# Mean over 8192 rows on one core: four small unused loads behind the first six groups, and a different last wait of SyncE

## The chip, the core and the metric

The kernel runs on one core of a Trainium2 chip. The metric is the device time of one execution in microseconds (us), so lower is better. The profile of one execution gives a slightly shorter figure, the span from the first to the last instruction of the program: 626.3 us, where that execution took 628.09 us.

## The reference

```python
def setup_inputs():
    return {"x": np.random.randn(8192, 8192).astype(np.float32)}

def reference(x):
    return np.mean(x, axis=0)
```

All 8192 rows of an 8192-column matrix of float32 are averaged: 268.44 MB are read from memory and 32 KB are written. Each number that is read enters one addition.

## The kernel before

The rows are read in 64 groups of 128 (G = 64, P = 128); a group is one row per partition, 4 MB. `bufs` holds six groups: slots 0 to 3 take the loads, slot 4 (`both`) and slot 5 (`acc`) the sums. VectorE adds groups until a few are left, TensorE adds the last ones over the partitions with a matrix of 1/8192, ScalarE and VectorE copy the results out of PSUM, and five small stores write them.

All loads are issued by SyncE, through one helper. A load is a DMA; it tells of its end through one of eight semaphores, taken in turn. The helper takes away the dependencies that the new load has on earlier loads (`declare_no_dep`), apart from two that it names in every second load, `over`.

```python
    def landed(*inss):
        nop = tc.keep_in_program_order(nc.sync.nop()).ins
        for o in inss:
            tc.add_manual_dep(nop, o.name, sync, reason="SyncE waits")

    def load(dst, src):
        ins = tc.keep_in_program_order(nc.sync.dma_start(out=dst, in_=src)).ins
        k = len(loads)
        over = loads[k - 8:k - 6] if k >= 8 and k % 2 == 0 else []
        tc.declare_no_dep(ins, group="loads", keep=over, reason="the reader of the buffer waited")
        for o in over:
            tc.add_manual_dep(ins, o.name, sync, reason="covers the next load too")
        tc.add_to_no_dep_group("loads", ins)
        loads.append(ins)
        return ins
```

The start: a part of a late group that is kept in `early`, four groups in one load, two groups in a second, and another part of a late group in `early`. Two large additions on VectorE bring the six groups down to one. The loop then loads two groups at a time into two free slots and adds them.

```python
    load(early[:, 5 * F:], rows(G - 4)[:, 14 * F:])
    first, second = load_rows(0, 0, 4), load_rows(4, 4, 2)
    load(early[:, :5 * F], rows(G - 1)[:, 9 * F:14 * F])
    add(bufs[:, 2:4, :], bufs[:, 2:4, :], bufs[:, 0:2, :], [first])
    add(bufs[:, 4:6, :], bufs[:, 4:6, :], bufs[:, 2:4, :], [second])
    add(acc, acc, both, [])
    # ... (warm-up of ScalarE)
    g = 6
    while g < G - 8:
        u = (g + 2) % 4
        dma = load_rows(g, u, 2)
        add(both, bufs[:, u, :], bufs[:, u + 1, :], [dma])
        add(acc, acc, both, ahead)
        # ... (GpSimd adds what lies in early at g = 24 and 32)
        g += 2
```

The end, cut: the last groups are loaded in pieces, summed by TensorE, copied and stored. The last store comes from SyncE and writes 2 KB out of `tail`, which VectorE copied from PSUM. Behind it SyncE waits for loads and stores that nothing else waited for; the remaining waits are added by the framework at the end of the program.

```python
    nc.vector.tensor_copy(out=tail[:], in_=last[:])
    landed(*joins.values())
    s5 = store(nc.sync, part(9, 14), res5[0:P:32, :], *loads[-7:-3])
    s0 = store(nc.sync, part(0, 4), res[0:P:32, 0, :])
    s2 = store(nc.scalar, part(14, 16), res2[0:P:32, :])
    store(nc.sync, part(8, 9), tail[0:P:32, :])
    landed(*loads[-3:-1])
    landed(loads[-1], s1)
    landed(s0, s5)
    landed(s2)
    hold = tc.keep_in_program_order(nc.vector.nop()).ins
    tc.add_manual_dep(hold, s0.name, sync, reason="VectorE ends late")
```

Of the kernel before, what the change touches and what calls it, by code (L numbers as in the profile page):

```python
# [9 lines left out]
def kernel(  # L10
# [27 lines left out]
    nc = tc.nc  # L38
    f32 = mybir.dt.float32
    M, N = x.shape  # L40
    P = nc.NUM_PARTITIONS
# [6 lines left out]
    sb = ctx.enter_context(tc.tile_pool(name="sb", bufs=1))  # L48
# [4 lines left out]
    acc = bufs[:, U - 1, :]  # L53
    ones = sb.tile([P, 32], f32, name="ones")
    early = sb.tile([P, 7 * F], f32, name="early")
    tail = sb.tile([P, W], f32, name="tail")
    warm = sb.tile([P, 32], f32, name="warm")
    nc.gpsimd.memset(ones[:], 1.0 / M)  # L58
    ready = sb.tile([P, 1], f32, name="ready")
    tc.keep_in_program_order(  # L60
# [3 lines left out]
    two = psp.tile([P, 2 * W], f32, name="two")  # L64
    last = psp.tile([P, W], f32, name="last")

    loads = []
# [18 lines that stand above are left out]
    def rows(g, n=1):  # L86
        return x[g * P:(g + n) * P, :]

    def load_rows(g, u, n):
        return load(bufs[:, u:u + n, :], rows(g, n).rearrange("(p j) c -> p j c", j=n))  # L90
# [3 lines left out]
    def add(dst, a, b, dmas):  # L94

        ins = nc.vector.tensor_add(out=dst, in0=a, in1=b).ins  # L96
        if dmas and adds:
            waiter = nc.scalar if len(adds) % 8 > 1 else nc.gpsimd
            nop = joins[waiter] = tc.keep_in_program_order(waiter.nop()).ins  # L99
            for o in dmas + adds[-1:]:  # L100
                tc.add_manual_dep(nop, o.name, sync, reason="the no-op waits")
            for group in ("loads", "adds"):
                tc.declare_no_dep(ins, group=group, reason="the no-op waited")
            tc.add_manual_dep(ins, nop.name, sync, reason="waits for both at once")
        elif adds:
            tc.declare_no_dep(ins, group="loads", reason="the add ahead waited")
        tc.declare_no_dep(ins, group="early", reason="the no-op waited, or the add behind it")
        tc.add_to_no_dep_group("adds", ins)
        adds.append(ins)

    load(early[:, 5 * F:], rows(G - 4)[:, 14 * F:])
    first, second = load_rows(0, 0, 4), load_rows(4, 4, 2)
    load(early[:, :5 * F], rows(G - 1)[:, 9 * F:14 * F])
    add(bufs[:, 2:4, :], bufs[:, 2:4, :], bufs[:, 0:2, :], [first])
    add(bufs[:, 4:6, :], bufs[:, 4:6, :], bufs[:, 2:4, :], [second])
# [4 lines left out]
    while g < G - 8:  # L120
# [5 lines left out]
        if g in (24, 32):  # L126
            lo, hi = (0, 4) if g == 24 else (4, 7)
            cols = slice((9 + lo) * F, (9 + hi) * F)
            ins = tc.keep_in_program_order(nc.gpsimd.tensor_add(  # L129
                out=acc[:, cols], in0=acc[:, cols], in1=early[:, lo * F:hi * F])).ins  # L130
# [8 lines left out]
    for lo, hi, loaded in [(0, 14, 14), (7, 16, 16)]:  # L139
        row = bufs[:, (g + 2) % 4, :]  # L140
        dma = load(row[:, :loaded * F], rows(g)[:, :loaded * F])
        cols = slice(lo * F, hi * F)
        add(acc[:, cols], acc[:, cols], row[:, cols], [dma])
        g += 1
    r61, r62, r63 = [bufs[:, (g + 1 + j) % 4, :] for j in range(3)]
    load(r62, rows(g))
    for cols in [slice(14 * F, 16 * F), slice(8 * F, 9 * F)]:
        tc.keep_in_program_order(nc.gpsimd.tensor_add(  # L148
            out=acc[:, cols], in0=acc[:, cols], in1=r62[:, cols]))
    g += 1  # L150
    for lo, hi in [(4, 8), (0, 4), (14, 16), (8, 9)]:
        load(r63[:, lo * F:hi * F], rows(g)[:, lo * F:hi * F])
# [27 lines left out]
    spread(two, r63, 14, 16)  # L180
    spread(last, r63, 8, 9)
    for n, (dst, q, c, cols) in enumerate(sums):
        tc.keep_in_program_order(nc.tensor.matmul(  # L183
            out=dst[32 * q:32 * q + 32, c:c + cols.shape[1]],
            lhsT=ones[:],
            rhs=cols,
            start=all((d is dst, k, at) != (True, q, c) for d, k, at, _ in sums[:n]),
            stop=all((d is dst, k, at) != (True, q, c) for d, k, at, _ in sums[n + 1:]),
            tile_position=(0, 32 * q),
            skip_group_check=True,  # L190
        ))

    res = both[:, :2 * F].rearrange("p (b c) -> p b c", b=2)
    res5 = both[:, 2 * F:2 * F + 5 * W]
    res2 = both[:, 4 * F:4 * F + 2 * W]

    def copy(dst, src):
        tc.keep_in_program_order(nc.scalar.copy(out=dst, in_=src))  # L198

    def store(engine, dst, src, *then):  # L200
        ins = tc.keep_in_program_order(engine.dma_start(out=dst, in_=src)).ins
        for o in then:
            tc.add_manual_dep(ins, o.name, sync, reason="follows that load")
        return ins

    def part(lo, hi):
        return out[lo * F:hi * F].rearrange("(q c) -> q c", q=4)

    copy(res[:, 1, :], banks[1][:])
    s1 = store(nc.scalar, part(4, 8), res[0:P:32, 1, :], loads[-4])  # L210
    copy(res5, wide[:, :5 * W])
    copy(res[:, 0, :], banks[0][:])
    copy(res2, two[:])
    nc.vector.tensor_copy(out=tail[:], in_=last[:])  # L214
    landed(*joins.values())
    s5 = store(nc.sync, part(9, 14), res5[0:P:32, :], *loads[-7:-3])
    s0 = store(nc.sync, part(0, 4), res[0:P:32, 0, :])
    s2 = store(nc.scalar, part(14, 16), res2[0:P:32, :])
    store(nc.sync, part(8, 9), tail[0:P:32, :])
    landed(*loads[-3:-1])  # L220
    landed(loads[-1], s1)
    landed(s0, s5)
    landed(s2)
    hold = tc.keep_in_program_order(nc.vector.nop()).ins
    tc.add_manual_dep(hold, s0.name, sync, reason="VectorE ends late")

# [29 lines left out]
```

## Time and profile before

| what | value |
|---|---|
| time, median of 2 runs (lowest to highest) | 628.41 us (628.39 to 628.43) |
| span of the profiled execution | 626.3 us |
| granted TensorE clock | 0.999 |
| VectorE busy | 529.3 us, 85% of the span |
| TensorE, ScalarE, GpSimd busy | 13.6, 3.7 and 12.0 us |
| read from memory, mean rate over the span | 268.44 MB, 429 GB/s |

The page of a profile gives, for each engine, the share of the span in which it was busy; then the same in 40 equal slices, with the busy share of the 16 DMA engines and what they moved; the DMA queues; the chain of work that ended last, followed back from the last instruction; and the groups of instructions. Other views answer questions: which wait of an engine or of SyncE's queue was ended by what, the instructions in order of time, and the issues of DMAs with the time until they landed. SyncE (SP) is a sequencer alone and has no busy time; its entries, marked SPq, are the instructions that issue a DMA. In the order of time the first two numbers are the start and the duration in us from the span's start, and entries that follow one another with the same form are merged.

### The profile page before, as it was taken

Reading aid. Unit: us, or ns where it says so; the run is one execution under the profiler, and the core shown is the slowest. Engines: PE = TensorE matmul, PEld = TensorE weight load, DVE = VectorE, ACT = ScalarE, POOL = GpSimd, SP = SyncE. Lnnn points to the kernel's source line nnn. Section 1 sums busy time; section 2 is a strip of 40 time slices with the busy share of each in tenths; the row PEclk is TensorE's granted clock in tenths of the full one; section 3 lists DMA queues with packets and bytes.
Section 4 is the critical chain, followed back from the end, with each engine's and each line's share of the span. In section 5 each row is a group of like instructions: output and inputs, shape, how many; then the busy total and the mean of one; then the engine's idle time right before and its main releaser. Section 6 shows DMA issues by size and latency. Waiting matters only on the chain.

```text
span 626.3 us, 483 instructions
## 1 busy us (share of the span) xinstructions
PE 13.6 (2%) x126; PEld 4.2 (1%) x126; DVE 529.3 (85%) x60; ACT 3.7 (1%) x6; POOL 12.0 (2%) x10
## 2 busy tenths in 40 slices
PE   0000000000000000000000000000000000000008
PEld 0000000000000000000000000000000000000002
DVE  0028999998888998889998899888898888999992
ACT  0000000000000000000000000000000000000001
POOL 0000000000000000020000200000000000000002
PEclk9999999999999999999999999999999999999999
DMA  9999999999999999999999999999999999999997
GB/s 381 456 402 429 458 431 439 406 465 402 469 402 469 402 469 402 469 402 469 402 469 402 456 414 448 423 423 448 402 469 402 469 402 469 402 435 435 428 434 297
DMA packets 5931, 268.50 MB, mean 429 GB/s; under 512 B 661, under 2 KB 669, under 8 KB 1065
## 3 DMA queue, kind: packets, MB, share of 16 engines
q1 hardware_dynamic: 5912, 268.46, 99.3%
q8 instruction: 1, 0.02, 0.0%
q10 hardware_dynamic: 16, 0.01, 0.0%
q14 instruction: 2, 0.01, 0.0%
HBM read 268.44 MB, written 0.03 MB: 429 GB/s over the span
## 4 chain that ended last, share of the span: by engine, by line
DMA 56%; DVE 31%; another core or an unknown queue 10%; PE 2%; issue 0%; ACTq 0%; POOL 0%; POOLq 0%
DMA bufs<-in_x_dram 56%; DVE bufs L96 31%; PE bank L183 2%; PE wide L183 0%; PE two L183 0%; PE last L183 0%; ACTq L99 0%; DVE tail L214 0%; POOL ready L61 0%; POOLq L99 0%; POOL ones L58 0%; POOLq L240 0%
## 5 line engine op out<-in xcount | busy, mean ns | idle before, releaser
L96 DVE TENSOR_TENSOR bufs<-bufs 128x8192 f32<-128x8192 f32 (+3 forms) x59 | 529.0, 8966 | 85.8 <-DMA bufs<-in_x_dram 43.1
L183 PE MATMUL bank<-bufs,ones 128*32 128x512 f32 x62 | 10.3, 769 | 609.9 <-DVE bufs L96 609.9
L129 POOL TENSOR_TENSOR bufs<-bufs,early 128x2048 f32<-128x2048 f32 (+1 forms) x2 | 7.9, 3954 | 348.4 <-DVE bufs L96 348.4
L148 POOL TENSOR_TENSOR bufs<-bufs 128x1024 f32<-128x1024 f32 (+1 forms) x2 | 3.6, 1820 | 259.0 <-DMA bufs<-in_x_dram 259.0
L214 DVE COPY tail<-last 128x128 f32<-128x128 f32 x1 | 0.3, 291 | 8.8 <-PE last L183 8.8
L183 PEld LDWEIGHTS bank<-bufs,ones 128*32 128x32 f32 x62 | 2.4, 130 | 616.1 <-issue 614.4
L198 ACT COPY bufs<-bank 128x512 f32<-128x512 f32 x2 | 1.2, 585 | 617.8 <-PE bank L183 617.8
L183 PE MATMUL wide<-bufs,ones 128*32 128x512 f32 (+1 forms) x32 | 2.5, 432 | 0.0
L117 ACT ACT_TABLE_LOAD x1 | 1.3, 1283 | 0.7 <-PEq L240 0.7
L183 PE MATMUL two<-bufs,ones 128*32 128x256 f32 x16 | 1.3, 385 | 0.0
L183 PEld LDWEIGHTS wide<-bufs,ones 128*32 128x32 f32 x32 | 1.0, 110 | 1.8 <-issue 1.8
L183 PE MATMUL last<-bufs,ones 128*32 128x128 f32 x16 | 0.8, 279 | 0.0
L198 ACT COPY bufs<-wide 128x640 f32<-128x640 f32 x1 | 0.7, 692 | 1.1 <-PE wide L183 1.1
L183 PEld LDWEIGHTS last<-bufs,ones 128*32 128x32 f32 x16 | 0.4, 109 | 1.1 <-issue 0.6
L183 PEld LDWEIGHTS two<-bufs,ones 128*32 128x32 f32 x16 | 0.4, 109 | 0.1
L198 ACT COPY bufs<-two 128x256 f32<-128x256 f32 x1 | 0.4, 372 | 0.1
L117 ACT COPY warm<-ones 128x32 f32<-128x32 f32 x1 | 0.2, 218 | 0.0
L61 POOL TENSOR_TENSOR ready<-ones 128x1 f32<-128x1 f32 x1 | 0.2, 193 | 0.1
L58 POOL MEMSET ones<- 128x32 f32 x1 | 0.1, 124 | 0.3 <-POOLq L240 0.3
L240 POOL MEMSET const-float32-0.0<- 128x1 f32 x1 | 0.1, 98 | 0.2 <-issue 0.2
L240 POOL MEMSET const-bfloat16-1.0<- 128x1 bf16 x1 | 0.1, 101 | 0.0
L240 POOL MEMSET const-uint8-127<- 128x1 uint8 x1 | 0.1, 101 | 0.0
(1 smaller groups left out, 0.1 us busy)
## 6 DMA issues: line engine op xcount, KB each, us to landing
bufs<-in_x_dram SPq DMA_DIRECT2D x6, 4096.0 KB, 20.4
bufs<-in_x_dram SPq DMA_DIRECT2D x1, 3584.0 KB
bufs<-in_x_dram SPq DMA_DIRECT2D x2, 1024.0 KB, 18.7
early<-in_x_dram SPq DMA_DIRECT2D x1, 1280.0 KB
early<-in_x_dram SPq DMA_DIRECT2D x1, 512.0 KB
bufs<-in_x_dram SPq DMA_DIRECT2D x1, 512.0 KB, 19.5
bufs<-in_x_dram SPq DMA_DIRECT2D x27, 29.9
bufs<-in_x_dram SPq DMA_DIRECT2D x1, 256.0 KB, 19.7
```

Of the source, the lines that this page charges most:

```text
L58: nc.gpsimd.memset(ones[:], 1.0 / M)
L61: nc.gpsimd.tensor_add(out=ready[:], in0=ones[:, 0:1], in1=ones[:, 1:2]))
L96: ins = nc.vector.tensor_add(out=dst, in0=a, in1=b).ins
L117: tc.keep_in_program_order(nc.scalar.copy(out=warm[:], in_=ones[:]))
L129: ins = tc.keep_in_program_order(nc.gpsimd.tensor_add(out=acc[:, cols], in0=acc[:, cols], in1=early[:, lo * F:hi * F])).ins
L148: tc.keep_in_program_order(nc.gpsimd.tensor_add(out=acc[:, cols], in0=acc[:, cols], in1=r62[:, cols]))
L183: tc.keep_in_program_order(nc.tensor.matmul(out=dst[32 * q:32 * q + 32, c:c + cols.shape[1]], lhsT=ones[:], rhs=cols, start=all((d is dst, ...
L198: tc.keep_in_program_order(nc.scalar.copy(out=dst, in_=src))
L214: nc.vector.tensor_copy(out=tail[:], in_=last[:])
L240: nc = _bacc.Bacc("TRN2", target_bir_lowering=False, num_devices=1)
```

## The change

Behind the load of groups 4 and 5, SyncE issues four more loads, of 2, 4, 8 and 12 rows, 64 bytes a row, all into a new tile `spare` that nothing reads. They don't go through the helper `load`. They change how the packets and the semaphores of the loads behind them are laid out: the small loads use fewer DMA engines than a load of 128 rows, and they take four of the turns of the eight semaphores.

At the end the waits of SyncE are regrouped: the no-ops behind the last store now wait also for the last instruction of GpSimd (`joined`), of ScalarE (`copied`), of TensorE (`summed`) and of VectorE (`ended`), so that of all waits the framework has only that for the last store itself left for SyncE's drain.

```diff
+    spare = sb.tile([P, 16], f32, name="spare")
 ...
     load(early[:, 5 * F:], rows(G - 4)[:, 14 * F:])
     first, second = load_rows(0, 0, 4), load_rows(4, 4, 2)
+    for n in (2, 4, 8, 12):
+        tc.keep_in_program_order(nc.sync.dma_start(out=spare[0:n, :], in_=rows(0)[0:n, 0:16]))
     load(early[:, :5 * F], rows(G - 1)[:, 9 * F:14 * F])
 ...
-        tc.keep_in_program_order(nc.gpsimd.tensor_add(
-            out=acc[:, cols], in0=acc[:, cols], in1=r62[:, cols]))
+        joined = tc.keep_in_program_order(nc.gpsimd.tensor_add(
+            out=acc[:, cols], in0=acc[:, cols], in1=r62[:, cols])).ins
 ...
-        tc.keep_in_program_order(nc.tensor.matmul(
+        summed = tc.keep_in_program_order(nc.tensor.matmul(
 ...
-    copy(res2, two[:])
-    nc.vector.tensor_copy(out=tail[:], in_=last[:])
+    copied = copy(res2, two[:])
+    ended = nc.vector.tensor_copy(out=tail[:], in_=last[:]).ins
 ...
     store(nc.sync, part(8, 9), tail[0:P:32, :])
-    landed(*loads[-3:-1])
-    landed(loads[-1], s1)
+    landed(loads[-2], joined)
+    landed(loads[-1], copied)
     landed(s0, s5)
-    landed(s2)
+    landed(s1, summed)
+    landed(s2, ended)
```

(Cuts are marked with "..."; the other lines of the change only keep the names of instructions for these waits.)

More of the change, by code (lines that the diff above doesn't have):

```diff
@@ L190 @@
             skip_group_check=True,
-        ))
+        )).ins
     res = both[:, :2 * F].rearrange("p (b c) -> p b c", b=2)
@@ L197, in copy @@
     def copy(dst, src):
-        tc.keep_in_program_order(nc.scalar.copy(out=dst, in_=src))
+        return tc.keep_in_program_order(nc.scalar.copy(out=dst, in_=src)).ins
     def store(engine, dst, src, *then):
```

## The prediction

> **What bounds the kernel now.** I began with the page's slices, then the DMA part, then the waits of SyncE's queue, and last the order of time at the two ends.
>
> ```profile
> DMA  9999999999999999999999999999999999999997
> GB/s 381 456 402 429 458 431 439 406 465 402 469 402 469 402 469 402 469 402 469 402 469 402 456 414 448 423 423 448 402 469 402 469 402 469 402 435 435 428 434 297
> ...
> HBM read 268.44 MB, written 0.03 MB: 429 GB/s over the span
> ...
> bufs<-in_x_dram SPq DMA_DIRECT2D x27, 29.9
> ```
>
> The sixteen DMA engines are busy nine tenths or more in 39 of 40 slices. The jumps between 402 and 469 GB/s are a matter of which slice a 64 KB packet is booked in; the mean is what counts. The trace's packet records give 2.418 us to a packet of 65536 bytes, so one engine moves 27.1 GB/s and sixteen move 433.6 GB/s; 268.44 MB then take 619.1 us. Between the first packet at 1.76 us and the end of the last load's packets at 623.28 us there is no stretch of 0.15 us without a packet. So the span of 626.3 us is 1.8 us of start, 621.5 us of unbroken reading, and 3 us of copies, stores and end. VectorE, 85% busy, only follows. The rule for any change here: **a pause in the reading is paid in full, because the rest already runs at the engines' rate and can't catch up.**
>
> Whether a pause can arise depends on how far SyncE issues ahead:
>
> ```profile
> engine line waited for: us in total, times, longest us
> SPq L76 <- DVE bufs L96: 587.1, 31, 57.7
> ```
>
> ```profile
> 0.74 0.39 SPq L76 DMA_DIRECT2D early<-in_x_dram  x1
> ...
> 1.19 0.92 SPq L76 DMA_DIRECT2D bufs<-in_x_dram  x2
> ...
> 2.15 0.43 SPq L76 DMA_DIRECT2D early<-in_x_dram  x1
> 43.06 17.22 DVE L96 TENSOR_TENSOR bufs<-bufs 128x16384 f32<-128x16384 f32 x1 [43.06 <-DMA bufs<-in_x_dram]
> 60.31 0.33 SPq L76 DMA_DIRECT2D bufs<-in_x_dram  x1
> 62.46 17.22 DVE L96 TENSOR_TENSOR bufs<-bufs 128x16384 f32<-128x16384 f32 x1 [2.17 <-POOLq L99]
> ```
>
> The first lines are SyncE's waits, the second view the order of time from 0 to 70 us (start, duration, what). Four loads are issued by 2.6 us. Then SyncE waits for a buffer, and issues the load of groups 6 and 7 at 60.31, when the first addition has ended. The trace's semaphore events say when the loads land: the four groups at 42.6 to 43.0, groups 4 and 5 at 61.9 to 62.4, the second part of `early` (1.25 MB) at 65.1 to 65.5. So at 60.31 the queue still holds about 1.2 us of groups 4 and 5 and 3.2 us of `early`. That `early` load is the bridge over which the stream passes to the next load. From there on each load of two groups is issued 29.9 us before it lands, though its packets take 19.4 us (landings at 84.9, 104.2, 123.6): some 10 us of cushion.
>
> **What the Trainium skill says.** Four places bear on this.
> - "DMA: Bandwidth & Descriptors", "Anatomy of one DMA": DMA engines do not wait on semaphores, the issuing sequencer does, before dispatch. A waiting SyncE therefore holds back every load behind it. The trace agrees: the loads start in program order and the issue of 60.31 follows the addition's end. The section also puts a fixed cost of about 2 us on one DMA of the GpSimd path, mostly the receipt that the data has landed. The nearest thing here, the last store (2 KB, from SyncE), is issued at 623.85 and landed at 625.47: 1.62 us.
> - Same page, "Latency and other measured facts": about 0.6 us to the first byte for SyncE's DMAs. Here the first issue runs from 0.74 to 1.13 and the first packet starts at 1.76: 0.63 us after its end, 1.02 us after its start.
> - Same page, "Why a DMA increments its semaphore by 16 and not by 1": a DMA uses as many engines as the largest number up to 16 that divides its rows, the lowest-numbered ones. So 2, 4, 8 and 12 rows go to as many engines, each with one packet per load. The stores of four rows show four landings each; loads of 2, 8 or 12 rows no run has shown yet.
> - Same page, "Where 436 GB/s comes from": a ceiling of 435.2 GB/s. The 433.6 above lies just under it, so the stream has nothing to gain.
>
> **The change part by part.**
>
> *The small loads as traffic.* Row n takes 64 bytes. The two busiest engines get four of the small packets, each with a 4-byte completion packet of 0.009 us (from the packet records). A 512-byte packet took 0.025 us, so this is at most 4 × 0.034 = 0.14 us on two engines. Skewing the engines by that much changes nothing: they are 0.4 us apart anyway (landings from 61.93 to 62.40).
>
> *The small loads as waits.* This is where I choose. All four write overlapping rows of one tile, `spare[0:n]`, and nothing takes the dependency away. The kernel's own `load()` does so for loads that reuse a buffer, with the words "the reader of the buffer waited": without those words a later load into the same place waits for the earlier one. The small loads have no such words. So the second waits for the first to land, the third for the second, the fourth for the third, and SyncE does the waiting, with the `early` load and the load of groups 6 and 7 behind it. Step by step, from rows of the trace before:
> 1. The first small load is issued at about 2.1 and runs behind groups 4 and 5. It lands with them, about 62.3.
> 2. The second is issued at 62.35. One small round trip: the last three stores of SyncE took 1.80, 1.67 and 1.62 us from start of issue to landing; I take 1.7 and 0.05 for SyncE to notice. It lands at 64.05.
> 3. The third is issued at 64.1 and lands at 65.8.
> 4. The fourth is issued at 65.85. Nothing behind it waits for it; its issue takes about 0.5 us (those stores: 0.64, 0.51, 0.50).
> 5. `early` is issued at 66.4, and its first packet starts 1.02 us later, at 67.4. In the kernel before it started at 61.54, right behind groups 4 and 5.
>
> The reading stands still for 67.4 − 61.54 = **5.8 us**, apart from 24 small packets. The load of groups 6 and 7 is then issued at 66.9, under the 3.2 us of `early`, so no second pause follows; the load behind it still waits for the addition that ends at 79.7, while its queue now lasts to about 90. Everything later shifts by 5.8 us.
>
> *The end.* After the last store landed (its four increments at 625.39 to 625.47), SyncE still ended one semaphore instruction at 625.51, then the drain at 625.54, and its barrier at 625.60. The change moves the waits for the other engines' last instructions ahead, so the drain itself waits for the store. One instruction of about 0.06 us leaves the path. The store's start, set by VectorE's copy at 623.53 to 623.82, doesn't move.
>
> Sum: 628.41 + 5.8 − 0.06 = **634.1 us**, 0.9% slower.
>
> **The rivals.**
> - *No wait arises* (overlapping writes without a reader left unordered, or queue order taken as enough). Then the small loads hide in the stream: 628.41 + 0.1 − 0.06, about 628.4. For it speaks that the change looks like a way to spread the engines apart. Against it, the explicit words in `load()`. I give it one chance in twelve.
> - *Round trips on an empty queue are dearer.* At 2.0 us each the pause is 6.4 us and the time 634.7. At 1.4 us, if a 64-byte read is quicker than the stores, it is 5.2 us and 633.5.
> - *The pause hides behind the 10 us cushion.* That cushion is one of issue, and exists only later; at 62 us the queue is empty. A stream at 433.6 GB/s can't make up time, so I don't believe it. It would give 628.4 too.
> - *VectorE becomes the bound.* It needs 17.4 us per pair of groups (two additions of 8.7) against 19.4 of reading, and a late load only makes it wait. The pause is not multiplied.
> - *The end gains more.* Less than 0.2 us lies between the last landing and SyncE's barrier, so no such gain can offset a pause.
>
> **Range and chances.** Round trips of 1.4 to 2.2 us, a first landing between 62.0 and 62.6, and 0.1 us of measurement give 633.2 to 635.5; I widen it downwards to 632.8 for a quicker first packet and upwards to 635.8. The hidden rival lies outside. Two per cent is 12.6 us, which no rival reaches: a pause would need round trips of 5 us, and a gain would need the stream to beat its rate. So within 2% gets 0.97, slower 0.02, faster 0.01.
>
> **What would show it.** In the order of time around 62 us: four short issues to `spare`, the second at about 62.3 and the others about 1.75 us apart, then `early` at about 66.4. SyncE's waits must list DMA `spare`, two or three times, the longest near 60 us. The fifth slice of the page (62.6 to 78.3 us) must fall from 458 to about 300 GB/s, and later landings must be 5.8 us later by a constant. If instead all five issues stand between 2 and 5 us, the ordering step was wrong and the time stays near 628.4. If the pause is there but the span grew by much less, the claim that nothing catches up was wrong.

## The result, and the profile after

The changed kernel took 633.38 us (median of 2 runs, 633.37 to 633.40) against 628.41 us: a ratio of 1.0076, 95% interval 1.0056 to 1.0097. In five rounds later on it took 633.44 us against 628.47 us, ratio 1.0077 (1.0064 to 1.0089). So it is some 5 us, or 0.8%, slower; 634.1 us was predicted.

The slices of the page after, for the DMA engines (the span is 631.6 us, so a slice is 15.8 us):

```profile
DMA  9998899999999999999999999999999999999997
GB/s 390 440 436 361 349 465 398 465 398 465 398 465 398 465 407 457 436 427 452 411 465 398 465 398 465 398 465 398 465 398 465 403 461 427 436 421 432 420 443 296
```

The hole is in the fourth and fifth slices (47.4 to 79.0 us), which held 429 and 458 GB/s before, and nowhere else. The waits of SyncE's queue in the kernel after (waited for: us in total, times, longest) name the new one:

```profile
SPq L77 <- DVE bufs L97: 529.0, 30, 21.4
SPq L115 <- DMA spare<-in_x_dram: 61.9, 3, 59.8
```

Line 115 is the line of the small loads, and it waits three times, once for 59.8 us. The kernel before spent those 58 us too, but in waiting for VectorE, with `early` already in the queue. The order of time after (start, duration, what):

```profile
2.15 63.15 SPq L115 DMA_DIRECT2D spare<-in_x_dram  x4
...
62.45 25.95 DVE L97 TENSOR_TENSOR bufs<-bufs 128x16384 f32<-128x16384 f32 x2 [2.22 <-POOLq L100]
65.35 0.36 SPq L77 DMA_DIRECT2D early<-in_x_dram  x1
65.83 33.44 SPq L77 DMA_DIRECT2D bufs<-in_x_dram  x3
```

The first line merges the four small issues: they begin at 2.15 and end 63 us later. The load of `early`, issued at 2.15 before, now goes out at 65.35, and that of groups 6 and 7 at 65.83 and not at 60.31. By then groups 4 and 5 had long landed (62.0 to 62.4 in the trace's semaphore events), and the sixteen engines had nothing but 24 packets of 64 bytes to move. The first packet of `early` starts at 66.33; before, it started at 61.54.

### The profile page after: what moved, and what is told of

Read it like the earlier page. It is cut to its first block, busy times and chain, and to the rows that moved or that the text cites. A ratio compares the mean times of both kernels' runs of the same rounds, so it can differ in the third digit from the quotient of the medians.

```text
span 631.6 us, 490 instructions
## 1 busy us (share of the span) xinstructions
PE 13.3 (2%) x126; PEld 4.5 (1%) x126; DVE 529.3 (84%) x60; ACT 3.7 (1%) x6; POOL 12.0 (2%) x10
## 4 chain that ended last, share of the span: by engine, by line
DMA 64%; DVE 24%; another core or an unknown queue 9%; PE 1%; SPq 0%; issue 0%; ACTq 0%
DMA bufs<-in_x_dram 64%; DVE bufs L97 24%; PE bank L186 1%; DMA spare<-in_x_dram 0%; PE wide L186 0%; SPq L77 0%; PE two L186 0%; SPq L115 0%; PE last L186 0%; ACTq L100 0%; DVE tail L217 0%
```

## The experiments

**No overlap.** Each small load gets columns of its own; packets, bytes, number of engines and turns of the semaphores stay.

```diff
-    spare = sb.tile([P, 16], f32, name="spare")
+    spare = sb.tile([P, 64], f32, name="spare")
-    for n in (2, 4, 8, 12):
-        tc.keep_in_program_order(nc.sync.dma_start(out=spare[0:n, :], in_=rows(0)[0:n, 0:16]))
+    for i, n in enumerate((2, 4, 8, 12)):
+        tc.keep_in_program_order(nc.sync.dma_start(
+            out=spare[0:n, 16 * i:16 * i + 16], in_=rows(0)[0:n, 0:16]))
```

> The changed kernel, but each of the four small loads has 16 columns of spare of its own, so none writes where another writes. Rows, bytes, the number of DMA engines each uses and the turns of the eight semaphores stay. Theory (the second, third and fourth small load wait for the one ahead and SyncE stands still): without overlap no wait arises, all five issues end by about 5 us, groups 4 and 5 are followed by early without a pause, and the time is 628.3 to 628.5 us. Rival A (short loads on few of the sixteen engines hurt the stream by themselves, through skew or their own handling): still 632 to 633.5. Rival B (the shifted turns of the semaphores make later loads wait): still 632 to 633.5.

Measured: 628.56 us against 628.47, ratio 1.0001 (0.9993 to 1.0009). Its order of time:

```profile
2.16 1.32 SPq L115 DMA_DIRECT2D spare<-in_x_dram  x4
3.52 0.36 SPq L77 DMA_DIRECT2D early<-in_x_dram  x1
...
60.44 0.35 SPq L77 DMA_DIRECT2D bufs<-in_x_dram  x1
```

All four issues take 1.32 us together, `early` follows at 3.52, and the next load at 60.44 as ever. The 5 us are gone with the overlap alone, so neither the traffic nor the shifted semaphores cost more than the 0.6 us that the interval leaves open. In the trace the reading ends as in the kernel before: the last load landed at 622.99 us in both.

**The end alone.** The four small loads and `spare` are left out of the changed kernel.

```diff
-    for n in (2, 4, 8, 12):
-        tc.keep_in_program_order(nc.sync.dma_start(out=spare[0:n, :], in_=rows(0)[0:n, 0:16]))
```

> The regrouped waits at the end alone, without any small load. Theory: between the last store's landing and SyncE's barrier about 0.05 us less than in the kernel before (0.137 there, 0.088 in the changed kernel), so 628.35 us, which the measurement may not part from 628.41. Rival (the regrouping delays the end, since the waits for other engines come behind one another): up to 0.5 us more than before, 628.9.

Measured: 628.19 us against 628.47, ratio 0.9995 (0.9987 to 1.0003). The trace has 0.09 us from the last store's landing (625.605) to SyncE's barrier (625.695), where the kernel before has 0.14. That is the gain that was meant, but it is not shown: of the eleven traces with this end seven have 0.08 to 0.13 us there, and four have 0.47 to 0.62 us. One of the four is the run without overlap above. It took 0.37 us more than this one (628.56 against 628.19), which the intervals don't resolve, and its trace has 0.47 us at that place.

**The small loads alone.** The kernel before with the four overlapping loads and its old end.

```diff
     first, second = load_rows(0, 0, 4), load_rows(4, 4, 2)
+    for n in (2, 4, 8, 12):
+        tc.keep_in_program_order(nc.sync.dma_start(out=spare[0:n, :], in_=rows(0)[0:n, 0:16]))
```

> The four small loads alone, with overlapping rows as in the change; the end as in the kernel before. Theory: the whole 5 us are here, 633.4 us. Rival (the end's part carries some of it): clearly below 633.

Measured: 633.58 us, ratio 1.008 (1.0066 to 1.0094). The whole cost is here.

**The changed kernel again**, without an edit.

> The changed kernel once more, in five rounds beside the kernel before, because the profiled spans differ by 5.3 us (631.6 against 626.3) and the measured times by 4.97 us. Theory: the same pause in every execution, 633.4 to 633.8 us.

Measured: 633.44 us, as said above. Its round trips were a little shorter (`early` issued at 65.16), and its span is 631.4 us.

**One wait, three waits, seven waits.** The list of rows is cut, and doubled.

```diff
-    for n in (2, 4, 8, 12):
+    for n in (2, 4):                              # first run
+    for n in (2, 4, 8, 12, 2, 4, 8, 12):          # second run
```

> The changed kernel with the first two small loads only (2 and 4 rows): one wait instead of three. Theory: in the changed kernel SyncE issued the second small load at 62.28, the third at 63.53, the fourth at 65.01 and early at 65.35; without the third and fourth, early is issued at about 62.6, 2.7 us sooner, so 633.4 - 2.7 = 630.7 us. Rival (the cost is a fixed price of any pause, not of the number of round trips): near 633.

> The changed kernel with eight small loads in the same place (2, 4, 8, 12 and again 2, 4, 8, 12 rows), all into overlapping rows: seven waits. Theory: four more round trips. Those seen took 1.23 us (4 rows), 1.46 (8 rows) and 1.35 (12 rows); with 1.2 for 2 rows and 0.02 for each wake-up the early load goes out 5.3 us later than in the changed kernel: 638.7 us. Rival (part of the later pause is absorbed by the cushion of the loads behind): below 637.

Measured: 630.69 us, ratio 1.0036 (1.0023 to 1.0049), and 639.02 us, ratio 1.0167 (1.015 to 1.0184). First the order of time with two small loads, then with eight:

```profile
62.31 0.25 SPq L115 DMA_DIRECT2D spare<-in_x_dram  x1
62.61 0.36 SPq L77 DMA_DIRECT2D early<-in_x_dram  x1
```

```profile
62.25 8.21 SPq L115 DMA_DIRECT2D spare<-in_x_dram  x7
70.51 0.36 SPq L77 DMA_DIRECT2D early<-in_x_dram  x1
```

`early` goes out at 62.61 or 70.51, 7.90 us later. In the traces the load of groups 6 and 7 lands at 87.51 or 95.43, 7.92 us later: the delay of this one issue is paid one for one, and nothing behind it makes up for it. The times differ by 639.02 − 630.69 = 8.33 us. In the trace with eight small loads, the slowest of that kernel's four executions (639.87 us), the loads behind lost another 0.9 us.

**A wait without a small load.** SyncE waits for groups 4 and 5 to land, and nothing is added to the queue.

```diff
-    for n in (2, 4, 8, 12):
-        tc.keep_in_program_order(nc.sync.dma_start(out=spare[0:n, :], in_=rows(0)[0:n, 0:16]))
+    landed(second)
```

> The changed kernel with no small load at all; in their place a single wait of SyncE for the load of groups 4 and 5 to land, ahead of the load of early. Theory (the wait does it, not the small loads): that load lands at 62.4, early is issued at 62.45, 2.9 us sooner than in the changed kernel, so about 630.5 us, 2.1 us slower than before with not one packet added. Rival (small loads are needed for the cost): 628.4.

Measured: 630.57 us against 628.49, ratio 1.0035 (1.0022 to 1.0048). Its order of time:

```profile
62.37 0.33 SPq L77 DMA_DIRECT2D early<-in_x_dram  x1
62.74 0.43 SPq L77 DMA_DIRECT2D bufs<-in_x_dram  x1
```

2.1 us are lost with not one byte more. The small loads only lengthen what the wait begins.

**The same chain on ScalarE's queue.** The small loads still overlap and wait for one another, but ScalarE issues them and waits.

```diff
     tc.keep_in_program_order(nc.scalar.copy(out=warm[:], in_=ones[:]))
+    for n in (2, 4, 8, 12):
+        tc.keep_in_program_order(nc.scalar.dma_start(out=spare[0:n, :], in_=rows(0)[0:n, 0:16]))
```

> The changed kernel with the same four overlapping small loads issued by ScalarE, behind its warm-up copy, and not by SyncE. They still wait for one another, but ScalarE does the waiting. Theory (what costs is that SyncE stands still while the queue of large loads runs dry): all five large loads go out as in the kernel before and the time is 628.2 to 628.6 us. Rival (a chain of small dependent loads beside the stream costs by itself): 630 or more.

Measured: 628.45 us, ratio 1.0001 (0.9993 to 1.0009). Its order of time:

```profile
0.90 0.52 ACTq L120 DMA_DIRECT2D spare<-in_x_dram  x1
...
2.15 0.52 SPq L77 DMA_DIRECT2D early<-in_x_dram  x1
3.16 18.15 ACTq L120 DMA_DIRECT2D spare<-in_x_dram  x3
```

The chain takes from 0.90 to past 21 us and harms nobody, for SyncE has issued `early` at 2.15. What costs is not a chain of small loads but which engine stands still for it.

**Behind a cushion.** The four loads move into the loop, behind the load of groups 20 and 21, where the next load is issued some 10 us before it is needed; then behind groups 40 and 41.

```diff
         dma = load_rows(g, u, 2)
+        if g == 20:                               # g == 40 in the second run
+            for n in (2, 4, 8, 12):
+                tc.keep_in_program_order(nc.sync.dma_start(
+                    out=spare[0:n, :], in_=rows(0)[0:n, 0:16]))
```

> The four overlapping small loads not at the start but in the loop, behind the load of groups 20 and 21, where every load is issued some 10 us before the queue runs out. Theory: the first small load lands only when all that stands ahead of it in the queue has been moved, so the cushion is used up whatever its size; the same pause, 633.4 us. Rival (the cushion of 10 us is larger than the 3 us of the round trips and hides them): 628.4 us.

> As the run with the small loads behind groups 20 and 21, but behind groups 40 and 41. That run came out at 634.5 us where 633.4 was expected: the stream restarted 4.8 us late like the changed kernel's, but its next load landed 5.7 us late (5.3 there), and from then on it moved 432.7 GB/s where the others move 433.5. If restarting with loads of 64 KB packets is what costs more, the next load again lands about 5.7 us late, and the slower rate now lasts half as long: about 634.2 us. If it was chance of that place or run, 633.4 us.

Measured: 634.50 us, ratio 1.0096 (1.0081 to 1.0111), and 634.69 us, ratio 1.0097 (1.0083 to 1.0111). SyncE's waits, then the order of time, of the first:

```profile
SPq L126 <- DMA spare<-in_x_dram: 31.0, 3, 29.1
```

```profile
220.56 2.87 SPq L126 DMA_DIRECT2D spare<-in_x_dram  x3
...
223.53 6.18 SPq L77 DMA_DIRECT2D bufs<-in_x_dram  x2
```

SyncE waits 29.1 us: the small load stands behind two loads of two groups and lands with the second, and the next load goes out at 223.53, when the queue is empty. The cushion of 10 us is used up. The theory holds in kind. In size the first run came out 1.1 us above its number, and the second 0.5 us above its own. The traces show four parts (taking a load as landed with the last of its sixteen landings, and comparing with the kernel before):

- The loads ahead of the small ones were already 0.25 and 0.33 us late.
- The pause cost 5.5 and 5.9 us, where it cost 5.3 us in the changed kernel: the landings on its two sides stand 24.85 and 25.23 us apart, not 19.36. The first packets of 64 KB behind it took 2.45 to 3.32 us, not 2.42.
- The loads further behind lost another 0.3 and 0.1 us.
- SyncE's barrier came 0.62 us after the last store's landing in both, not 0.09 as in the changed kernel.

So a restart with 64 KB packets may cost 0.2 to 0.6 us more than one with the 10 KB packets of `early`; the rest of the excess has other places.

**A bare wait in the loop**, in the same place, on the kernel with the new end alone:

```diff
         dma = load_rows(g, u, 2)
+        if g == 20:
+            landed(dma)
```

> The kernel with the new end and no small load, in which SyncE waits for the load of groups 20 and 21 to land before it issues the next. Theory: a bare wait costs the same wherever it stands, since it empties the queue: 630.6 us like the bare wait at the start; if restarting with 64 KB packets costs more, as the run behind groups 20 and 21 suggests, up to 631.6 us. Rival (the cushion of 10 us absorbs a wait of 2 us): 628.4 us.

Measured: 630.93 us against 628.50, ratio 1.0039 (1.0024 to 1.0055), 0.36 us above the bare wait at the start, which their intervals don't part. The next load landed at 241.7 to 242.2 us, 2.4 to 2.5 us later than before, and by the last loads this had grown to 3.0 us. The cushion absorbs nothing here either.

## Why the prediction was right

The mechanism held at every step, and two sizes were off in opposite directions: that they offset each other in part, 1.0 us too much against 0.5 us left out, was luck.

- *Who waits.* The ordering between overlapping writes exists, in three waits of SyncE; without the overlap the cost is zero. The rival without a wait, given one chance in twelve, named the right time for that case (628.4; 628.56 measured).
- *The first landing.* The second small load was issued at 62.28 (62.35 predicted).
- *The round trip* is the term that was mis-sized: 1.7 us from the 2 KB to 10 KB stores. The trace has 1.23 us for 4 rows (62.28 to 63.52) and 1.46 for 8 (63.53 to 65.00); the second run of the same kernel has 1.22 and 1.26. A small load's issue takes 0.25 to 0.30 us where the stores took 0.50 and more, which is more than half of the difference over the two round trips and nearly all of it in the fourth issue. The rival of 1.4 us was nearer. Hence `early` at 65.35, not 66.4.
- *The restart* was missing from the sum. The first packet of `early` came 66.33 − 61.54 = 4.79 us late (5.8 predicted), but `early` had landed 5.32 us later than before (70.84 against 65.52): its first dozen packets of 10240 bytes took 0.86 to 1.18 us each, where they take 0.385 us in an unbroken stream. So 4.8 + 0.5 in the profile in place of 5.8 + 0. The bare wait at the start shows the same 0.5: first packet 1.81 us late (63.35), `early` landed 2.3 us late (67.84).
- *Nothing catches up.* The load of groups 6 and 7 landed 5.3 us late, and the last store landed at 630.76 against 625.47, again 5.3. The spans grew by 5.3 us and the median time by 4.97, because the profiled execution of the kernel before was 0.32 us faster than its median: 633.40 − 628.09 = 5.31 us.
- *The end.* One instruction did leave the path, and the trace has 0.05 us less from landing to barrier (0.06 predicted). But the four traces with 0.47 to 0.62 us at that place have more than the two with the old end (0.14 each). Why SyncE is late there is open, and so is whether the old end can be late too. The changed kernel's trace also shows that the framework has more left than the wait for the last store: ahead of SyncE's drain stand two more waits, for loads.
- *The end of the reading* was misread, without weight in the sum: the loads' last packets ended at 622.53 and the last load landed at 622.99. What ended at 623.28 is a packet of 16 KB in another queue, which the page lists as "q8 instruction".
- *The slice.* 349 GB/s where about 300 was foretold: the pause was 4.8 us and not 5.8, the longer span moves the borders, and a part of the hole falls into the slice before it (361 GB/s).

What stays open is why the stream loses more over the loads behind some pauses and nothing behind others. It lost 0.9 us with eight small loads, 0.5 and 0.3 us with the bare wait in the loop and at the start, 0.3 and 0.1 us in the two runs behind a cushion, and nothing in the changed kernel or with two small loads. A pause is not needed for it: in the first run behind a cushion two loads well ahead of the small ones stood 19.43 and 19.60 us apart, not 19.35. How the sixteen engines stand to one another then may matter; no run tested that.

## What to carry to other kernels

Ask of each new wait of the engine that issues the stream what stands in the queue behind it: a wait for the transfer at the queue's tail empties the queue, even where the next load would have had a lead of 10 us, and costs the round trip and the restart in full where the stream is the bound (2.1 and 2.4 us here for a bare wait). Scratch loads that nobody reads still write, so overlapping ones are a chain; give each its own columns, or let an idle engine issue them. The regrouping of the waits at the end took one instruction of some 0.05 us off the path, and no comparison of times showed it.

## What the runs showed of the hardware

Two things were not expected, and one was confirmed. A small load from SyncE's queue on idle engines comes back in 1.2 to 1.5 us; the same load from ScalarE's queue beside the stream of 64 KB packets took 7.7 to 9.2 us (issues at 3.16, 11.75 and 21.01 us, the last landing at 28.67), one engine's packet lasting 2.42 us. A stream that has stood still starts with longer packets: the first dozen of 10 KB took 0.86 to 1.18 us, not 0.385, and in the three runs with a pause in the loop the first sixteen of 64 KB took 2.45 to 3.41 us, not 2.42. Confirmed is that the number of engines follows the rows: the trace has 2, 4, 8 and 12 landings for the four loads, as the Trainium skill says in "DMA: Bandwidth & Descriptors", "Why a DMA increments its semaphore by 16 and not by 1".
